# Behind the last linear scores: rotary keys next to the query latent, weights rounded ahead of tanh, the late gates' products first

## The chip, the cores and the metric

The kernel runs on one core of one Trainium2 chip. The metric is the device time of one execution in microseconds (us); the median of three runs is given, and lower is better. A profile is one more execution, taken with the hardware profiler.

## The reference

One transformer block for 512 tokens of width 1024, in float32. A norm and one wide linear layer give eleven pieces; a gated linear attention (GLA, 4 heads, two directions) and a latent attention (MLA, 8 heads) use them, and two gates mix the two. Then come an output layer, a second norm and a two-layer MLP.

```python
proj = rmsnorm(h, g_mix) @ w_in
(gq, gk, gv, gr, z_gf, z_gb, cq, ckv, kr, z_ma, z_mb) = split(proj)
y_gla = gla_branch(gq, gk, gv, gr, z_gf, z_gb, ...)       # scores, masked, times v, both directions
y_mla = mla_branch(cq, ckv, kr, positions, ...)
    # q = rmsnorm(cq) @ w_uq, its last 32 columns of each head rotated by the position
    # k_nope, v = rmsnorm(ckv) @ w_ukv;  k_rope = rope(kr), one for all heads
    # softmax(q k^T / sqrt(96)) v
merged = sigmoid(z_ma) * y_gla + sigmoid(z_mb) * y_mla
h = h + merged @ w_out
h = h + square(relu(rmsnorm(h) @ w_ff1)) @ w_ff2
out = rmsnorm(h)
```

## The kernel before

Tokens lie along the free axis (512) and features on the 128 partitions. Every float32 product is made of three matmuls (`mm3`, lines 88 to 90): each operand is split into a rounded part (h) and a remainder (l), and h·h, h·l and l·h are summed in PSUM. `split` (lines 92 to 94) makes the two parts: ScalarE rounds (line 93), then VectorE, or GpSimd where a caller says so, subtracts (line 94). Weights come through a stage of three SBUF buffers ("wf"): SyncE requests the next weight when the buffer's last reader is done.

PSUM holds two sets of four banks. The set "mm" takes products, "at" takes scores and the linear attention's outputs. A product that finds no free bank makes TensorE wait until the last reader of the oldest one is done.

The program runs in stages: the first linear layers, the linear attention head by head, the latents between them, then the latent attention (32 steps of scores, softmax, transposes and values), the output layer, and the MLP. The stage that matters here begins behind the scores of the last linear head (h = 3; `sc = gla_scores(...)`). Each engine works through its instructions in program order: the calls to `in_program_order` pin ScalarE, VectorE and TensorE to the order in which the code is written, with only TensorE moved in a few places. So what an engine does next is what the code says next, and one instruction that waits holds all behind it on its engine.

In this stage the code does the following, with names as in the profile:

- `zb5 = proj_run(...)` is a gate product; `gated` (lines 368 to 374) multiplies it by R, the reciprocal norm of each token, on VectorE (line 371), and makes tanh of half of it on ScalarE (line 373). tanh needs another function table than the sine before it (`ACT_TABLE_LOAD`).
- `cq_.normed()` splits the query latent (cqhl, lines 801 to 805); `rotary.tables()` makes sin and cos (lines 837, 838).
- `rotary_begin()` loads and splits two weights for the rotary queries (wr0, wr1), in two stage buffers.
- `ckv_.diagonals()` and `ckv_.spread()` prepare the norm of the key/value latent (ckvr, ckvdg, then ckvrs in PSUM); `ckv_.normed()` applies it and splits the result (ckvc, ckvhl).
- `begin(C_ZB + 6 * P, "zb6")` loads and splits the weights of gate 6; `begin(... "zb7")` those of gate 7.
- `gla_turn` transposes a finished linear head (y) and copies it out on ScalarE (yg, line 753); `gla_out` is the product of the last linear head (gla3o); `gla_squares` makes its squares on ScalarE (line 729), `gla_gated` the gated output on VectorE (grb, grc, line 740).
- `rotary_k()` rotates the keys on VectorE (lines 871 to 874), splits them (kbuf) and has SyncE copy them to three other key buffers (line 881).
- `rotary_q()` rotates the queries (roa, rob, ro; lines 860 to 862), and `up_units(0)` makes queries (wq0, uq, q), keys (wk0, uk) and values (uv) of the first two attention heads, a piece at each `next(units)`; the second piece asks SyncE for the copies of the rotary queries (line 1024).

On TensorE the order is: zb5, y, gla3o, ckvrs, the two rotary query products (ro), zb6, uq, uk, uv in two halves, zb7, the first attention scores (s).

Of the kernel before, what the change touches and what calls it, by code (L numbers as in the profile page):

```python
# [18 lines left out]
P = 128  # L19
# [16 lines left out]
C_ZA, C_ZB = 3776, 4800  # L36
# [20 lines left out]
def tile_block(ctx: ExitStack, tc: tile.TileContext, t, out: bass.AP):  # L57
# [6 lines left out]
    def tl(shape, dt, tag, bufs, name):  # L64
        serial[0] += 1
        return sb.tile(shape, dt, tag=tag, bufs=bufs, name=f"{name}_{serial[0]}")

    def u2(name, dt=F32, shape=(P, S)):
        return tl(list(shape), dt, "u2", 29, name)

    def u4(name, dt=F32R, shape=(P, 2, S)):
        return tl(list(shape), dt, "u4", 26, name)

    def sm(name, n=4, dt=F32):
        return tl([P, n], dt, "sm", 24, name)

    def ps(tag, name):
        serial[0] += 1
        return pp.tile([P, S], F32, tag=tag, bufs=4, name=f"{name}_{serial[0]}")
# [4 lines left out]
    def raw(x):  # L84
        return x.bitcast(F32)

    def mm3(acc, lh, ll, rh, rl, start, stop, onto=False):
        nc.tensor.matmul(acc, lh, rh, start=start, stop=False, skip_group_check=onto)  # L88
        nc.tensor.matmul(acc, lh, rl, start=False, stop=False, skip_group_check=onto)  # L89
        nc.tensor.matmul(acc, ll, rh, start=False, stop=stop, skip_group_check=onto)  # L90

    def split(hi, lo, src, rest=nc.vector):
        nc.scalar.activation(hi, src, AF.Copy)  # L93
        rest.tensor_tensor(lo, src, raw(hi), op=ALU.subtract)  # L94
# [12 lines left out]
    def traced():  # L107
        return len(nc.cur_bb.bb.instructions)
# [102 lines left out]
    def stage(nk, nw, name):  # L211
        wf = tl([P, nk, nw], F32, "wf", 3, f"{name}f")
        return wf

    def halves(nk, nw, name):
        wh = tl([P, nk, nw], F32R, "wh", 4, f"{name}h")
        wl = tl([P, nk, nw], F32R, "wl", 4, f"{name}l")
        return wh, wl
# [12 lines left out]
    def proj_begin(w, col, name, tag="mm"):  # L231
        wh, wl = weights(w[:, col : col + P], name)
        return wh, wl, ps(tag, name)

    def begin_late(col, name, tag="mm", w=None):

        wf = stage(KD, P, name)
        nc.sync.dma_start(wf, (w_in if w is None else w)[:, col : col + P].rearrange("(k p) w -> p k w", p=P))
        wh, wl = halves(KD, P, name)
        nc.scalar.activation(wh, wf, AF.Copy)  # L240

        def lows():
            nc.vector.tensor_tensor(wl, wf, raw(wh), op=ALU.subtract)

        return (wh, wl, ps(tag, name)), lows

    def proj_run(begun, src, half=None, ks=range(KD)):
        wh, wl, acc = begun
        c = slice(0, S) if half is None else slice(half * 256, half * 256 + 256)
        for k in ks:  # L250
            mm3(acc[:, c], wh[:, k, :], wl[:, k, :], src[k][:, 0, c], src[k][:, 1, c], k == 0, k == KD - 1)
        return acc
# [56 lines left out]
    xT = [u4(f"xT{k}") for k in range(KD)]  # L309
# [57 lines left out]

    def gated(acc, name):

        z = u2(f"z{name}")  # L370
        nc.vector.tensor_tensor(z, acc, R, op=ALU.mult)  # L371
        th = u2(f"t{name}")
        nc.scalar.activation(th, z, AF.Tanh, scale=0.5)  # L373
        return z, th

    def qk_normed(h, x, acc):
        n = u2(f"{'gq' if x == 0 else 'gk'}n{h}")
# [8 lines left out]
    g2 = [gated(f_accs[2 + x], f"b{x}")[1] for x in range(2)]  # L386
# [338 lines left out]
    def gla_squares(h, os):  # L725
        tot = sm(f"gla{h}ss")
        for i, o in enumerate(os):
            junk = u2(f"gla{h}sq")
            nc.scalar.activation(junk[:, 0:GDV], o, AF.Square, accum_out=tot[:, i : i + 1])
        nc.gpsimd.tensor_scalar(tot, tot, 1.0 / GDV, EPS, op0=ALU.mult, op1=ALU.add)  # L730
        nc.gpsimd.tensor_tensor(tot, tot, mhalf.to_broadcast([P, NT]), op=ALU.pow)
        nc.gpsimd.tensor_tensor(tot, tot, r_x, op=ALU.mult)
        return tot

    def gla_gated(h, os, rs):

        half, at = h // 2, (h % 2) * GDV
        for i, o in enumerate(os):
            g = g1[i, half][:, at : at + GDV]
            nc.vector.scalar_tensor_tensor(g, o, rs[:, i : i + 1], g, op0=ALU.mult, op1=ALU.mult)  # L740

    def gla_turn(h):

        half, at = h // 2, (h % 2) * GDV
        for dv in range(2):
            f = 2 * h + dv
            tp = ps("mm", f"y1{f}")
            for i in range(NT):
                nc.tensor.transpose(
                    tp[:, i * P : (i + 1) * P], g1[i, half][:, at + dv * P : at + (dv + 1) * P], ident  # L750
                )
            y = u2(f"yg{f}")
            nc.scalar.activation(y, tp, AF.Copy, scale=gla_gain[:, f : f + 1])
            y1.append(y)


    class Latent:
# [4 lines left out]
        def begin(self, j):  # L762
            self.begun[j] = proj_begin(w_in, self.col + j * P, f"{self.name}{j}")
# [77 lines left out]
    def rotary_begin():  # L841
        res = []
        for x in range(2):
            wf = stage(3, P, f"wr{x}")
            lo = NOPE + x * HALF
            for k in range(3):
                nc.sync.dma_start(
                    wf[:, k, :].rearrange("p (h e) -> p h e", h=MH), w_uq[:, k, :, lo : lo + HALF]
                )
            wh, wl = halves(3, P, f"wr{x}")  # L850
            split(wh, wl, wf)
            res.append((wh, wl))
        return res

    def rotary_q(accs):
        res = []
        for x in range(2):
            a, b = u2(f"roa{x}"), u2(f"rob{x}")
            ta, tb = (cos, sin) if x == 0 else (sin, cos)
            nc.vector.scalar_tensor_tensor(a, accs[0], QK_SCALE, ta, op0=ALU.mult, op1=ALU.mult)  # L860
            nc.vector.scalar_tensor_tensor(b, accs[1], QK_SCALE, tb, op0=ALU.mult, op1=ALU.mult)
            nc.vector.tensor_tensor(a, a, b, op=ALU.subtract if x == 0 else ALU.add)
            hl = u4(f"ro{x}")
            split(hl[:, 0, :], hl[:, 1, :], a)
            res.append(hl)
        return res

    def rotary_k():
        r = slice(64, 96)
        sgn = u2("krsin")  # L870
        nc.vector.tensor_scalar(sgn[r], sin[r], cst[r, K_SIGN : K_SIGN + 1], None, op0=ALU.mult)
        nc.vector.tensor_tensor(kswap[r], kswap[r], sgn[r], op=ALU.mult)
        nc.vector.tensor_tensor(kr[r], kr[r], cos[r], op=ALU.mult)
        nc.vector.tensor_tensor(kr[r], kr[r], kswap[r], op=ALU.add)
        res = []
        for b in range(4):
            kb = u4(f"kbuf{b}")
            if b == 0:
                split(kb[r, 0, :], kb[r, 1, :], kr[r])
            else:  # L880
                nc.sync.dma_start(raw(kb[r]), raw(res[0][r]))
            res.append(kb)
        return res
# [258 lines left out]
    ckv_, cq_ = Latent(C_CKV, 2, V_KV, "ckv"), Latent(C_CQ, 3, V_Q, "cq")  # L1142
# [73 lines left out]
    for h in range(GH - 1):  # L1216
# [5 lines left out]
        acc = latent.products(j)  # L1222
        if h < 2:
            w_b, lows = begin_late(C_GQ + (h + 2) * P, f"gq{h + 2}")
# [15 lines left out]
        os = gla_out(h, sc)  # L1240
        scaled_qk.within("b", gate.parts)
        rs = gla_squares(h, os)
# [11 lines left out]
        else:  # L1254
            zb = begin(C_ZB + 4 * P, "zb4")
# [4 lines left out]
            w_b = begin(C_ZB + 5 * P, "zb5")  # L1260
            zb = proj_run(zb, xT)

    h = GH - 1
    sc = gla_scores(*scaled_qk.parts())
    ckv_.sums()
    zb5 = proj_run(w_b, xT)
    cq = cq_.normed()
    cos, sin = rotary.tables()
    wr = rotary_begin()
    g2.append(gated(zb, "b4")[1])  # L1270
    g2.append(gated(zb5, "b5")[1])
    ckv_.diagonals()
    zb = begin(C_ZB + 6 * P, "zb6")
    gla_turn(h - 1)
    os = gla_out(h, sc)
    kbuf = rotary_k()
    ckv_.spread()
    rs = gla_squares(h, os)
    ckv = ckv_.normed()
    accs = [up_T(*w, cq, f"ro{x}") for x, w in enumerate(wr)]  # L1280
    units = up_units(0)
    next(units)
    ro = rotary_q(accs)
    gla_gated(h, os, rs)
    zb = proj_run(zb, xT)
    next(units)
    g2.append(gated(zb, "b6")[1])
    zb = begin(C_ZB + 7 * P, "zb7")
    first_units = traced()
    for _ in units:  # L1290
        pass
    first_units = first_units, traced()
    at = traced()
    zb = proj_run(zb, xT)
    last_gate = at, traced()
    g2.append(gated(zb, "b7")[1])
    in_program_order(fixed, SPLITTERS)
# [3 lines left out]
    units = up_units(1)  # L1301
# [5 lines left out]
    for n in range(4 * MH + LAG_C - 1):  # L1307
# [19 lines left out]
        if n in (6, 14):  # L1327
            units = up_units(n // 8 + 2)
# [4 lines left out]
        b = n - LAG_B  # L1333
# [45 lines left out]
    for i in range(NT):  # L1379
        r = u4(f"h{i}", F32, (P, D))  # L1380
# [186 lines left out]
    y, z = merged_sums(last, nc.vector)  # L1567
# [81 lines left out]
    for qd in range(NQ):  # L1649
# [14 lines left out]
        for n, m in enumerate(ORDER):  # L1664
# [4 lines left out]
            if m == 2:  # L1669
                accs, begin = [ps("mm", f"gw{qd}{rb}") for rb in range(2)], True  # L1670
# [3 lines left out]
            else:  # L1674
                accs, begin = (zs_, m == 5) if m in (5, 3) else (xs_, m == 1)
# [46 lines left out]
```

## Time and profile before

| | us |
|---|---|
| three runs | 763.59, 764.57, 764.74 (median 764.57) |
| the profiled execution | 766.85 |
| its span, first to last instruction | 764.8 |
| TensorE busy (matmul) | 751.8 (98%) |
| VectorE busy | 586.4 (77%) |
| ScalarE busy | 461.6 (60%) |
| GpSimd busy | 165.3 (22%) |
| mean granted clock of TensorE | 0.991 |

Engines are named PE (TensorE matmul), PEld (its weight loads), DVE (VectorE), ACT (ScalarE), POOL (GpSimd) and SP (SyncE, which requests transfers). L371 is line 371 of the kernel before. A timeline row has start, duration, engine, line, operation, output <- inputs, the shape and the number of merged instructions, and in brackets the idle time before it with who ended it. Buffer numbers are left out of names, so zb stands for each of the gates, and its neighbours tell which. Matmuls overlap: a row's duration is longer than the distance to the next one.

### The profile page before, as it was taken

How to read it: one execution, taken by the hardware profiler on the slowest of the kernel's cores; microseconds unless marked ns; L12 is line 12 of the kernel's file. 1: busy time of each engine (PE TensorE's matmuls, PEld its weight loads, DVE VectorE, ACT ScalarE, POOL GpSimd, SP SyncE). 2: the span in 40 equal slices, each digit the busy share in tenths (PEclk: the TensorE clock that was granted, in tenths of full speed). 3: DMA queues.
4: the chain of work that ended last, by engine and by line, in shares of the span. 5: the costliest groups of instructions: out<-in, count | busy, mean ns of one | idle time of the engine just before them, and what ended most of it. 6: DMA issues, size and time to landing. Idle time of an engine off the chain costs nothing.

```text
span 764.8 us, 10256 instructions
## 1 busy us (share of the span) xinstructions
PE 751.8 (98%) x3720; PEld 636.1 (83%) x3720; DVE 586.4 (77%) x850; ACT 461.6 (60%) x780; POOL 165.3 (22%) x238
## 2 busy tenths in 40 slices
PE   9999999999999997999999999999999999999996
PEld 7888887889889886889888988888888888888885
DVE  7777888789787575798997876965887478848795
ACT  7556565577567473898866775435653556346634
POOL 0722110262562512117662100000000000000014
PEclk9999999999999997999999999999999999999999
DMA  9849581711222233227989421363115510650002
GB/s 311 253 132 230 164 176 57 130 29 32 78 56 37 40 80 90 66 56 205 251 205 241 138 84 55 111 186 89 56 56 186 144 34 22 193 166 0 28 1 110
DMA packets 94306, 87.59 MB, mean 115 GB/s; under 512 B 15696, under 2 KB 66896, under 8 KB 94256
## 3 DMA queue, kind: packets, MB, share of 16 engines
q1 hardware_dynamic: 87760, 74.33, 32.5%
q0 software_dynamic: 6208, 12.32, 9.1%
q8 instruction: 29, 0.48, 0.3%
q10 hardware_dynamic: 288, 0.28, 0.1%
q14 instruction: 21, 0.17, 0.1%
HBM read 83.25 MB, written 2.10 MB: 112 GB/s over the span
## 4 chain that ended last, share of the span: by engine, by line
PE 90%; DVE 4%; ACT 3%; issue 1%; POOL 0%; POOLq 0%; ACTq 0%; DVEq 0%
PE f L88 8%; PE f L89 8%; PE f L90 8%; PE gx L88 4%; PE gx L89 4%; PE gx L90 4%; PE first L330 3%; PE gz L88 2%; PE gz L89 2%; PE gz L90 2%; PE tp L1081 1%; PE zb L88 1%; PE zb L89 1%; PE zb L90 1%; PE wox L88 1%
## 5 line engine op out<-in xcount | busy, mean ns | idle before, releaser
L1661 POOL DMA_DIRECT2D gfin<-in_g_final x1 | 0.6, 628 | 284.0 <-PE f L90 284.0
L951 DVE TENSOR_TENSOR w<-w,w 128x1024 f32<-128x1024 f32 x32 | 38.7, 1221 | 0.3
L1061 DVE TENSOR_REDUCE top<-s 128x1 f32<-128x512 f32 x32 | 21.8, 681 | 2.9 <-PE s L90 2.6
L1066 ACT ACTIVATE e<-s,top 128x512 f32<-128x512 f32 x32 | 22.0, 689 | 2.6 <-DVE top L1061 2.4
L94 DVE TENSOR_TENSOR pT<-tp,pT 128x512 fp32r<-128x512 f32 x32 | 21.6, 681 | 2.4 <-ACT pT L93 2.2
L1388 DVE TENSOR_TENSOR h<-h,gx 128x512 f32<-128x512 f32 x32 | 21.5, 682 | 1.9 <-PE gx L90 1.8
L93 ACT ACTIVATE pT<-tp 128x512 fp32r<-128x512 f32 x32 | 18.9, 597 | 3.2 <-PE tp L1081 3.1
L1081 PE MATMUL tp<-ident,e 128*128 128x128 f32 x128 | 19.3, 274 | 0.4 <-ACT e L1072 0.2
L88 PE MATMUL av<-pT,v 128*128 128x256 f32 x64 | 18.9, 296 | 0.0
L93 ACT ACTIVATE ghb<-y 128x512 fp32r<-128x512 f32 x16 | 10.1, 633 | 14.0 <-DVE y L897 14.0
L1454 ACT ACTIVATE fa<-f 128x512 f32<-128x512 f32 x32 | 18.5, 578 | 0.0
L1081 PEld LDWEIGHTS tp<-ident,e 128*128 128x128 f32 x128 | 15.1, 140 | 3.9 <-ACT e L1072 0.8
L89 PE MATMUL av<-pT,v 128*128 128x256 f32 x64 | 18.2, 285 | 0.0
L90 PE MATMUL av<-pT,v 128*128 128x256 f32 x64 | 18.2, 284 | 0.0
L540 ACT ACTIVATE bds<-bd 128x512 f32<-128x512 f32 x4 | 2.4, 598 | 20.9 <-PE bd L536 20.9
L93 ACT ACTIVATE b_00h<-w 128x1024 fp32r<-128x1024 f32 x7 | 7.4, 1059 | 12.6 <-PE gz L90 6.0
L373 ACT ACTIVATE tb<-zb 128x512 f32<-128x512 f32 x8 | 4.9, 631 | 16.5 <-DVE zb L371 16.5
L93 ACT ACTIVATE b_20h<-w 128x1024 fp32r<-128x1024 f32 x7 | 7.4, 1059 | 12.1 <-PE gz L90 6.0
L93 ACT ACTIVATE b_10h<-w 128x1024 fp32r<-128x1024 f32 x7 | 7.4, 1060 | 12.1 <-PE gx L90 6.0
L88 PE MATMUL s<-kbuf,q 96*128 96x512 f32 x32 | 14.2, 444 | 0.1
L1463 ACT ACTIVATE px<-fa 128x256 f32<-128x256 f32 x32 | 13.4, 418 | 1.0
L947 POOL DMA_DIRECT2D w<-in_w_out x10 | 12.2, 1398 | 6.5 <-DVE bo60l L94 5.3
(1731 smaller groups left out, 2956.2 us busy)
## 6 DMA issues: line engine op xcount, KB each, us to landing
w<-in_w_ff SPq DMA_DIRECT2D x64, 256.0 KB, 3.4
w<-in_w_out POOLq DMA_DIRECT2D x10, 512.0 KB, 9.0
grw<-in_w_in SPq DMA_DIRECT2D x8, 512.0 KB, 8.5
zaw<-in_w_in SPq DMA_DIRECT2D x8, 512.0 KB, 6.5
gvw<-in_w_in SPq DMA_DIRECT2D x8, 512.0 KB, 4.5
w<-in_w_out SPq DMA_DIRECT2D x16, 256.0 KB, 6.2
x<-in_xt SPq DMA_DIRECT2D x8, 256.0 KB, 5.3
vw<-in_w_first SPq DMA_DIRECT2D x8, 256.0 KB, 5.4
```

The source lines that it names most:

```text
L88: nc.tensor.matmul(acc, lh, rh, start=start, stop=False, skip_group_check=onto)
L89: nc.tensor.matmul(acc, lh, rl, start=False, stop=False, skip_group_check=onto)
L90: nc.tensor.matmul(acc, ll, rh, start=False, stop=stop, skip_group_check=onto)
L93: nc.scalar.activation(hi, src, AF.Copy)
L94: rest.tensor_tensor(lo, src, raw(hi), op=ALU.subtract)
L330: nc.tensor.matmul(f_accs[i], a[:, i * P : (i + 1) * P], b, start=k == 0 and x == 0, stop=k == KD - 1 and x == 2)
L951: nc.vector.tensor_tensor(wq[dst][g], wq[x][g], wq[y][g], op=op)
L1061: nc.vector.tensor_reduce(top, acc, axis=AX.X, op=ALU.max, negate=True)
L1066: nc.scalar.activation(e, acc, AF.Exp, bias=top, accum_out=tot[:, qt % 2 : qt % 2 + 1])
L1081: nc.tensor.transpose(tp[:, k * P : (k + 1) * P], e[:, k * P : (k + 1) * P], ident)
L1388: nc.vector.tensor_tensor(hc, hc, acc, op=op)
L1454: nc.scalar.activation(a, acc, AF.Relu)
```

## The change

The code of the stage is written in another order; nothing is added to what is computed and nothing left out. `gated` is cut into its product and its tanh, and `rotary_k` into rotation and split, so that the parts can stand apart. TensorE's and GpSimd's orders stay as they are.

```diff
     cq = cq_.normed()
     cos, sin = rotary.tables()
+    late = [over_rms(acc, f"b{f}") for f, acc in ((4, zb), (5, zb5))]
+    rotary_k()
+    ckv_.diagonals()
     wr = rotary_begin()
-    g2.append(gated(zb, "b4")[1])
-    g2.append(gated(zb5, "b5")[1])
-    ckv_.diagonals()
     zb = begin(C_ZB + 6 * P, "zb6")
+    kbuf = rotary_k_split()
+    g2 += [half_tanh(z, f"b{f}") for f, z in ((4, late[0]), (5, late[1]))]
     gla_turn(h - 1)
     os = gla_out(h, sc)
-    kbuf = rotary_k()
+    rs = gla_squares(h, os)
     ckv_.spread()
-    rs = gla_squares(h, os)
     ckv = ckv_.normed()
     accs = [up_T(*w, cq, f"ro{x}") for x, w in enumerate(wr)]
     units = up_units(0)
     next(units)
     ro = rotary_q(accs)
+    zb = over_rms(proj_run(zb, xT), "b6")
+    next(units)
+    w_b = begin(C_ZB + 7 * P, "zb7")
     gla_gated(h, os, rs)
-    zb = proj_run(zb, xT)
-    next(units)
-    g2.append(gated(zb, "b6")[1])
-    zb = begin(C_ZB + 7 * P, "zb7")
+    g2.append(half_tanh(zb, "b6"))
     first_units = traced()
     for _ in units:
         pass
     first_units = first_units, traced()
     at = traced()
-    zb = proj_run(zb, xT)
+    zb = proj_run(w_b, xT)
     last_gate = at, traced()
     g2.append(gated(zb, "b7")[1])
```

The new functions hold what `gated` and `rotary_k` held:

```python
    def over_rms(acc, name):
        z = u2(f"z{name}")
        nc.vector.tensor_tensor(z, acc, R, op=ALU.mult)
        return z

    def half_tanh(z, name):
        th = u2(f"t{name}")
        nc.scalar.activation(th, z, AF.Tanh, scale=0.5)
        return th
```

VectorE behind the query latent, before (wr0l and wr1l are the remainders of the rotary query weights, zb4 and zb5 the gate products, ckvr to ckvdg the diagonals, krsin and kswap the first steps of the rotary keys):

```order
L94 TENSOR_TENSOR wr0l_502_2573<-wr0f_500_2568,wr0h_501_2572 128x384
L94 TENSOR_TENSOR wr1l_505_2581<-wr1f_503_2576,wr1h_504_2580 128x384
L371 TENSOR_TENSOR zb4_506_2584<-zb4_475_2412,R_82 128x512
L371 TENSOR_TENSOR zb5_508_2588<-zb5_482_2455,R_82 128x512
L789 TENSOR_TENSOR ckvr_494_2524<-ckvr_494_2524,r_x_80 128x4
L791 CAST ckvrh_510_2593<-ckvr_494_2524 128x4
L792 TENSOR_TENSOR ckvrl_511_2594<-ckvr_494_2524,ckvrh_510_2593 128x4
L292 TENSOR_TENSOR ckvdg_512_2597<-ident_61,ckvrh_510_2593 128x512
L292 TENSOR_TENSOR ckvdg_512_2597<-ident_61,ckvrl_511_2594 128x512
L94 TENSOR_TENSOR zb6l_515_2603<-zb6f_513_2600,zb6h_514_2602 128x1024
L871 TENSOR_SCALAR krsin_523_2671<-sin_499_2565,gvec_78 32x512
L872 TENSOR_TENSOR kswap_66_353<-kswap_66_353,krsin_523_2671 32x512
```

And the same place now:

```order
L375 TENSOR_TENSOR zb4_500_2568<-zb4_475_2412,R_82 128x512
L375 TENSOR_TENSOR zb5_501_2570<-zb5_482_2455,R_82 128x512
L878 TENSOR_SCALAR krsin_502_2572<-sin_499_2565,gvec_78 32x512
L879 TENSOR_TENSOR kswap_66_353<-kswap_66_353,krsin_502_2572 32x512
L880 TENSOR_TENSOR kr_65_352<-kr_65_352,cos_498_2564 32x512
L881 TENSOR_TENSOR kr_65_352<-kr_65_352,kswap_66_353 32x512
L796 TENSOR_TENSOR ckvr_494_2524<-ckvr_494_2524,r_x_80 128x4
L798 CAST ckvrh_503_2578<-ckvr_494_2524 128x4
L799 TENSOR_TENSOR ckvrl_504_2579<-ckvr_494_2524,ckvrh_503_2578 128x4
L292 TENSOR_TENSOR ckvdg_505_2582<-ident_61,ckvrh_503_2578 128x512
L292 TENSOR_TENSOR ckvdg_505_2582<-ident_61,ckvrl_504_2579 128x512
L94 TENSOR_TENSOR wr0l_508_2590<-wr0f_506_2585,wr0h_507_2589 128x384
```

The gate products and the four steps of the rotary keys stand first; the rotary query weights' remainders, which stood first, follow the diagonals, and behind them come the remainders of zb6 and of the keys (kbuf).

ScalarE in the same place, before (wr1h and zb6h are rounded weights, tb4 and tb5 the tanh, yg the transposed head, kbuf0 the rounded rotary keys, gla3sq the squares):

```order
L93 ACTIVATE wr1h_504_2580<-wr1f_503_2576 128x384
L373 ACT_TABLE_LOAD
L373 ACTIVATE tb4_507_2586<-zb4_506_2584 128x512
L373 ACTIVATE tb5_509_2590<-zb5_508_2588 128x512
L93 ACTIVATE zb6h_514_2602<-zb6f_513_2600 128x1024
L753 ACTIVATE yg4_518_2612<-y14_517_2607,gla_gain_350 128x512
L753 ACTIVATE yg5_520_2619<-y15_519_2614,gla_gain_350 128x512
L93 ACTIVATE kbuf0_524_2676<-kr_65_352 32x512
L729 ACTIVATE gla3sq_530_2689,gla3ss_529_2688<-gla3o0_521_2621 128x256
```

And now:

```order
L93 ACTIVATE wr1h_510_2597<-wr1f_509_2593 128x384
L93 ACTIVATE zb6h_513_2603<-zb6f_512_2601 128x1024
L93 ACTIVATE kbuf0_516_2608<-kr_65_352 32x512
L380 ACT_TABLE_LOAD
L380 ACTIVATE tb4_520_2617<-zb4_500_2568 128x512
L380 ACTIVATE tb5_521_2619<-zb5_501_2570 128x512
L760 ACTIVATE yg4_523_2626<-y14_522_2621,gla_gain_350 128x512
L760 ACTIVATE yg5_525_2633<-y15_524_2628,gla_gain_350 128x512
L736 ACTIVATE gla3sq_529_2686,gla3ss_528_2685<-gla3o0_526_2635 128x256
```

The weights of zb6 and the keys are rounded ahead of the table load and tanh; the keys stood behind yg.

VectorE again, behind the rotary queries, before (ro1 ends the rotary queries, grb and grc are the gated head, zb6 the gate's product by R, zb7l the remainder of gate 7's weights, q00 and q01 the query remainders of the first two heads):

```order
L94 TENSOR_TENSOR ro1_549_2761<-roa1_547_2756,ro1_549_2761 128x512
L740 SCALAR_TENSOR_TENSOR grb_108_490<-gla3o0_521_2621,gla3ss_529_2688,grb_108_490 128x256
L740 SCALAR_TENSOR_TENSOR grb_109_491<-gla3o0_521_2621,gla3ss_529_2688,grb_109_491 128x256
L740 SCALAR_TENSOR_TENSOR grc_110_492<-gla3o1_522_2622,gla3ss_529_2688,grc_110_492 128x256
L740 SCALAR_TENSOR_TENSOR grc_111_493<-gla3o1_522_2622,gla3ss_529_2688,grc_111_493 128x256
L371 TENSOR_TENSOR zb6_552_2798<-zb6_516_2606,R_82 128x512
L94 TENSOR_TENSOR zb7l_556_2805<-zb7f_554_2802,zb7h_555_2804 128x1024
L98 SCALAR_TENSOR_TENSOR q00_550_2792<-uq0_558_2809,q00_550_2792 64x512
L98 SCALAR_TENSOR_TENSOR q01_551_2795<-uq0_558_2809,q01_551_2795 64x512
```

And now:

```order
L94 TENSOR_TENSOR ro1_549_2761<-roa1_547_2756,ro1_549_2761 128x512
L375 TENSOR_TENSOR zb6_550_2788<-zb6_515_2607,R_82 128x512
L94 TENSOR_TENSOR zb7l_555_2799<-zb7f_553_2796,zb7h_554_2798 128x1024
L747 SCALAR_TENSOR_TENSOR grb_108_490<-gla3o0_526_2635,gla3ss_528_2685,grb_108_490 128x256
L747 SCALAR_TENSOR_TENSOR grb_109_491<-gla3o0_526_2635,gla3ss_528_2685,grb_109_491 128x256
L747 SCALAR_TENSOR_TENSOR grc_110_492<-gla3o1_527_2636,gla3ss_528_2685,grc_110_492 128x256
L747 SCALAR_TENSOR_TENSOR grc_111_493<-gla3o1_527_2636,gla3ss_528_2685,grc_111_493 128x256
L98 SCALAR_TENSOR_TENSOR q00_551_2790<-uq0_558_2809,q00_551_2790 64x512
L98 SCALAR_TENSOR_TENSOR q01_552_2793<-uq0_558_2809,q01_552_2793 64x512
```

The gate's product and the remainder of gate 7's weights stand ahead of the four gatings; on ScalarE the rounding of zb7 stands ahead of the tanh of zb6. Among SyncE's requests one place changes: zb7's weights stood ahead of the three key copies (kbuf) and now stand behind them. The requests for the rotary queries stay where they were.

More of the change, by code (lines that the diff above doesn't have):

```diff
@@ L368, in gated @@
     def gated(acc, name):
+        z = over_rms(acc, name)
+        return z, half_tanh(z, name)
+    def over_rms(acc, name):
         z = u2(f"z{name}")
         nc.vector.tensor_tensor(z, acc, R, op=ALU.mult)
+        return z
+    def half_tanh(z, name):
         th = u2(f"t{name}")
         nc.scalar.activation(th, z, AF.Tanh, scale=0.5)
-        return z, th
+        return th
     def qk_normed(h, x, acc):
@@ L874, in rotary_k, with rotary_k_split @@
         nc.vector.tensor_tensor(kr[r], kr[r], kswap[r], op=ALU.add)
+    def rotary_k_split():
+        r = slice(64, 96)
         res = []
```

## The prediction

> **What bounds the kernel now.** I read three views in this order: the waits of TensorE, the granted clock by stretch, and the timeline of the stage behind the last linear scores. First the waits of TensorE over the whole span (waited for: us in total, times, longest):
>
> ```profile
> PE zb L88 <- DVE q L98: 2.2, 1, 2.2
> PE uv L88 <- DVE zb L371: 1.7, 1, 1.7
> ...
> PE tp L1081 <- ACT e L1072: 0.2, 1, 0.2
> ```
>
> Before its last instruction TensorE hardly waits but in two places, and both lie in this stage. So whatever is won there shortens the span, if nothing late follows. The same two in the timeline (start, duration, what is computed, and in brackets the idle time and who ended it), with the start of the attention scores behind them:
>
> ```profile
> 292.05 0.28 PE L90 MATMUL uv<-wk0h,ckvhl 128*128 128x256 f32 x1
> 294.07 0.39 PE L88 MATMUL uv<-wk0h,ckvhl 128*128 128x256 f32 x1 [1.74 <-DVE zb L371]
> 299.04 0.76 PE L88 MATMUL zb<-xT,zb7h 128*128 128x512 f32 x1 [2.23 <-DVE q L98]
> 307.17 0.40 PE L88 MATMUL s<-kbuf,q 96*128 96x512 f32 x1
> ```
>
> The second half of the values (uv) waits for the PSUM bank that gate zb6 holds until VectorE multiplies it by R. Gate zb7 waits for the bank of uq, free when VectorE has made the second head's query remainder (q L98). Then the clock, in stretches of 3.4 us (stretch, length, busy us of PE, PEld, DVE, ACT and POOL with counts, then granted clock, DMA share, GB/s):
>
> ```profile
> 290.90:294.30 3.40, 1.66 (x15) 1.46 (x14) 2.86 (x6) 0.42 (x2) 0.00 (x0) 1.00 0.55 156
> 294.30:297.70 3.40, 2.51 (x12) 2.21 (x11) 1.82 (x2) 2.00 (x4) 0.00 (x0) 0.50 0.12 19
> 301.10:304.50 3.40, 3.40 (x9) 2.63 (x9) 1.18 (x2) 1.66 (x6) 2.67 (x5) 0.50 0.28 40
> 304.50:307.20 2.70, 2.70 (x13) 2.21 (x13) 0.00 (x0) 0.00 (x0) 0.56 (x1) 0.99 0.71 239
> ```
>
> After the first wait the clock is at half until 304.5, so the 24 matmuls of zb7 take 307.17 - 299.04 = 8.13 us. Gate zb6, also 24 matmuls, shows their price at full clock, with two more starts on which the sum rests:
>
> ```profile
> 270.42 0.39 PE L90 MATMUL zb<-xT,zb5l 128*128 128x512 f32 x1
> 278.20 0.39 PE L90 MATMUL ro<-cqhl,wr0l 128*128 128x512 f32 x1
> 281.83 0.39 PE L88 MATMUL zb<-xT,zb6h 128*128 128x512 f32 x1
> 287.27 0.39 PE L88 MATMUL uq<-cqhl,wq0h 128*128 128x512 f32 x1
> ```
>
> 287.27 - 281.83 = 5.44 us, so the half clock costs zb7 2.7 us. Both waits end on VectorE, which is why its row is what the change has to shorten.
>
> **The change part by part.** VectorE's row in this stage:
>
> ```profile
> 268.08 1.89 DVE L805 TENSOR_TENSOR cqhl<-cqc,cqhl 128x512 fp32r<-128x512 f32 x3
> 271.84 0.56 DVE L94 TENSOR_TENSOR wr0l<-wr0f,wr0h 128x384 fp32r<-128x384 f32 x1 [1.86 <-ACT wr0h L93]
> 272.78 1.28 DVE L371 TENSOR_TENSOR zb<-zb,R 128x512 f32<-128x512 f32 x2
> 276.97 1.23 DVE L94 TENSOR_TENSOR zb6l<-zb6f,zb6h 128x1024 fp32r<-128x1024 f32 x1 [1.23 <-ACT zb6h L93]
> 278.23 0.48 DVE L871 TENSOR_SCALAR krsin<-sin,gvec 32x512 f32<-32x512 f32 x1
> 281.44 0.68 DVE L94 TENSOR_TENSOR kbuf<-kr,kbuf 32x512 fp32r<-32x512 f32 x1 [0.69 <-ACT kbuf L93]
> 282.15 1.29 DVE L801 TENSOR_TENSOR ckvc<-ckvc,ckvrs 128x512 f32<-128x512 f32 x2
> 284.89 0.69 DVE L860 SCALAR_TENSOR_TENSOR roa<-ro,cos 128x512 f32<-128x512 f32 x1
> ```
>
> It idles 1.86 + 1.23 + 0.69 us on ScalarE here. The new order fills the first gap and removes the others. VectorE is free at 268.08 + 1.89 = 270.0. The product of zb5 needs the matmul that ends at 270.42 + 0.39 = 270.8, so the two products (0.64 each) end at 271.5. Rotary keys (from 278.23 to the gap that ends at 281.44, so to 280.75, 2.5 us): 274.0. The diagonals (from the products' end, 274.06, to the gap that ends at 276.97, so 1.7 us): 275.7. Two rotary weight remainders (271.84 to 272.78, 1.0 us): 276.7. The remainder of zb6 (1.23): 277.9; of the keys (0.68): 278.6; the two latent products (1.29): 279.9. Then ScalarE decides, whose rows are:
>
> ```profile
> 270.68 0.71 ACT L838 ACTIVATE cos<-turns,half_pi 128x512 f32<-128x512 f32 x1
> 273.55 1.28 ACT L373 ACT_TABLE_LOAD   x1 [1.33 <-DVE zb L371]
> 274.84 1.16 ACT L373 ACTIVATE tb<-zb 128x512 f32<-128x512 f32 x2
> 276.84 1.25 ACT L753 ACTIVATE yg<-y,gla_gain 128x512 f32<-128x512 f32 x2
> 281.43 0.38 ACT L729 ACTIVATE gla3sq<-gla3o 128x256 f32<-128x256 f32 x1
> 283.00 1.16 ACT L803 ACTIVATE ckvhl<-ckvc 128x512 fp32r<-128x512 f32 x2
> 284.48 1.11 ACT L93 ACTIVATE wk0h<-wk0f 128x128 fp32r<-128x128 f32 x4
> ```
>
> Sine and cosine are ready at 271.4, in time. Rounding the keys now stands ahead of the table load and waits for them at 274.0: keys (the gap of 0.69 that they made on VectorE) 274.7, load 276.0, both tanh 277.1, both yg 278.4, squares (281.43 to 283.00) 279.9. There the latent's rounding begins; it began at 283.00. The first rotary query product began 1.89 us behind it, so it begins at 281.8, in place of 284.89, and its partner's matmuls end just then (281.83 in TensorE's rows). That is 3.1 us won.
>
> The table load is now on this chain. [...]
>
> Rounding zb6's weights ahead of tanh is worth nothing by itself: they were ready at 278.2 and are needed at 281.83. If that cover went, TensorE would wait for each late microsecond. That the copies of the rotary queries are requested earlier is worth nothing either; they keep their place among SyncE's transfers, behind wk1f. What moves on SyncE is a cost: stage buffers come free later. The rows (issue; then KB each, us to landing):
>
> ```profile
> 273.99 0.37 SPq L1007 DMA_DIRECT2D wk0f<-in_w_ukv  x1
> wk0f<-in_w_ukv SPq DMA_DIRECT2D x1, 384.0 KB, 5.4
> zb7f<-in_w_in SPq DMA_DIRECT2D x1, 512.0 KB, 4.0
> ```
>
> wk0f goes out 1.6 us behind the end of wr0l (272.40), now 276.3, so at 277.9, and lands at 283.3. Its four roundings (1.11) then hold ScalarE until 284.4, while the first rotary difference, three VectorE steps behind 281.8, is ready at 283.9: 0.5 us lost. A landing faster than 4.9 us makes that nothing, a slower one adds all of itself; I take the row's 5.4. zb7f now stands behind the three key copies, which wait for 278.6; going out near 281, it lands near 285, needed at 288. The late halves of the old row follow:
>
> ```profile
> 291.16 0.69 DVE L94 TENSOR_TENSOR ro<-roa,ro 128x512 fp32r<-128x512 f32 x1 [0.70 <-ACT ro L93]
> 291.77 0.87 DVE L740 SCALAR_TENSOR_TENSOR grb<-gla3o,gla3ss,grb 128x256 f32<-128x256 f32 x2
> 293.34 0.68 DVE L371 TENSOR_TENSOR zb<-zb,R 128x512 f32<-128x512 f32 x1
> 295.72 1.23 DVE L94 TENSOR_TENSOR zb7l<-zb7f,zb7h 128x1024 fp32r<-128x1024 f32 x1 [1.70 <-ACT zb7h L93]
> 296.86 0.68 DVE L98 SCALAR_TENSOR_TENSOR q<-uq,q 64x512 fp32r<-64x512 f32 x1
> 298.20 0.69 DVE L98 SCALAR_TENSOR_TENSOR q<-uq,q 64x512 fp32r<-64x512 f32 x1 [0.66 <-ACT q L97]
> ```
>
> Rotary queries take 284.89 to 291.85, 7.0 us: 281.8 + 7.0 + 0.5 = 289.3. Now zb6 comes first (0.6): 289.9, before TensorE reaches uv's second half at 292.05 + 0.12 = 292.2. **The first wait, 1.74 us, is gone.** Then zb7's remainder (1.23), whose rounding ScalarE does meanwhile, so that the 1.70 us wait goes: 291.1. The four gatings (291.77 to 293.34, 1.6): 292.7. The two query remainders (296.86 to 298.89, 2.0): 294.7. zb7 followed them by 0.15: **294.85 instead of 299.04, 4.2 us earlier.** uv's 12 matmuls at 0.12 end at 293.6, so a wait of about 1.25 us stays where 2.23 was.
>
> If that does not drop the clock, zb7 takes 5.44 instead of 8.13 us, 2.7 us more. **Sum: 4.2 + 2.7 = 6.9 us.** The profiled execution, 766.85 us with a span of 764.8, would become 760.0; the median of the runs lies 2.28 below it, so 764.57 - 6.9 = 757.7. If wk0f lands early: 757.2. If nothing of the second wait stayed (zb7 at 293.6): 299.04 - 293.6 + 2.7 = 8.1, so 756.4.
>
> **Rivals.** *The clock drops on the wait that stays.* For: one wait of 1.74 us did it, in a stretch with 1.66 of 3.40 us busy. Against: 1.25 us leaves a stretch nearly two thirds busy. Between 0.2 and 1.74 us this trace shows no wait behind which the clock could be read with certainty. The clock came back after one stretch that was all busy, so half clock would last 3.4 to 6.8 us and cost half of that, 1.7 to 3.4: 759.4 to 761.1. [...]
>
> *Late transfers take the wait's place.* wk0f or zb7f lands 3 us later, among the key copies: from 282.8 for wk0f and 288 for zb7f each microsecond goes to zb7's start. 757.7 + 2.5 and up to 3.4 of clock: 760 to 764.
>
> *Given back in the attention.* If that were bound by VectorE or ScalarE, an earlier start would be lost again: 763.1 to 766.1. Against: both stood idle ahead of it, VectorE over 5 us:
>
> ```profile
> 307.37 0.69 DVE L371 TENSOR_TENSOR zb<-zb,R 128x512 f32<-128x512 f32 x1 [5.09 <-PE zb L90]
> ```
>
> *Slower.* The remainder wr0l, moved behind rotary keys and diagonals, is ready at 276.3; TensorE reads it at 278.20. From a slip of 1.9 us, say of the tables or the key transfers, TensorE waits, and all of the chain behind it too. To be 1.5 us slower than before the wait must be 6.9 + 1.5 = 8.4 us, or 5.0 with the clock fallen: 766.1 and more. Nothing in the rows is that late.
>
> **How the numbers follow.** Forecast (756.4 to 759.2, clock up): 0.72. Clock drops: 0.13. Late transfers: 0.07. Given back: 0.05. Slower: 0.03. A measurement of this kernel tells about 0.2%, 1.5 us. Faster: 0.72 + 0.13 + 0.07 = 0.92 (the edge of late transfers within it), same 0.05, slower 0.03. The range takes the first two cases, and 0.4 us below them for the spread of single runs (763.59 to 764.74 before): 756.0 to 761.1.
>
> **What would show it.** Right: uv never waits, one wait of about 1.25 us ahead of zb7, granted clock 1.00 throughout, first rotary product about 3 us earlier, roundings of wk0 close behind its landing. Wrong: a wait ahead of ro or zb6, a clock of 0.50 behind uv, or waits of TensorE in the attention that weren't there.

## The result, and the profile after

| | before | after |
|---|---|---|
| median of the runs | 764.65 us (763.59 to 764.74, 4 runs) | 758.15 us (757.73 to 758.25, 4 runs) |
| the profiled execution | 766.85 | 758.25 |
| its span | 764.8 | 756.4 |
| mean granted clock | 0.991 | 0.998 |

The ratio of the medians is 0.9917, its 95% interval 0.99 to 0.9934: 5.0 to 7.6 us faster. 757.7 was forecast. First the waits of TensorE after the change (waited for: us in total, times, longest):

```profile
PE warm L320 <- POOL ident masks.py:199: 1.5, 1, 1.5
PE zb L88 <- DVE q L98: 0.6, 1, 0.6
PE zax L88 <- DVE zac L688: 0.4, 1, 0.4
PE tp L1091 <- ACT e L1082: 0.2, 1, 0.2
```

The wait of uv is gone, that of zb7 is 0.6 in place of 2.2 us, and no row is new in the attention. The stage in TensorE's timeline, from the first transposition of the finished head (y), through uv's second half and zb7, to the first scores:

```profile
269.62 0.38 PE L756 MATMUL y<-ident,grb 128*128 128x128 f32 x2
...
291.07 0.28 PE L88 MATMUL uv<-wk0h,ckvhl 128*128 128x256 f32 x1
...
292.39 0.28 PE L90 MATMUL uv<-wk0h,ckvhl 128*128 128x256 f32 x1
293.25 0.47 PE L88 MATMUL zb<-xT,zb7h 128*128 128x512 f32 x1 [0.58 <-DVE q L98]
298.80 0.40 PE L88 MATMUL s<-kbuf,q 96*128 96x512 f32 x1
```

And where the stage began before:

```profile
270.65 0.38 PE L749 MATMUL y<-ident,grb 128*128 128x128 f32 x2
```

From y to zb7 it is 293.25 - 269.62 = 23.63 us; before, 299.04 - 270.65 = 28.39: **4.76 us less**. zb7 itself, to the first scores, takes 5.55 in place of 8.13: **2.58 less**. Together 7.34 us. From the first scores to the end of the span it is 756.4 - 298.8 = 457.6 us after and 764.8 - 307.2 = 457.6 before: nothing of the gain is given back. The span is 8.4 us shorter; the 1.03 that are left lie ahead of the stage, in code that is the same in both. They arise in the first 8 us of the program, at the first matmuls of 512 columns, here before:

```profile
5.07 2.05 PE L330 MATMUL first<-xT,first0h 128*128 128x512 f32 x4
6.91 1.42 PE L330 MATMUL first<-xT,first0l 128*128 128x512 f32 x4
8.17 1.09 PE L330 MATMUL first<-xT,first0h 128*128 128x512 f32 x4
```

and after:

```profile
4.97 1.38 PE L330 MATMUL first<-xT,first0h 128*128 128x512 f32 x4
6.19 1.11 PE L330 MATMUL first<-xT,first0l 128*128 128x512 f32 x4
7.13 2.00 PE L330 MATMUL first<-xT,first0h 128*128 128x512 f32 x8
```

The first eight take 8.17 - 5.07 = 3.10 us before and 7.13 - 4.97 = 2.16 after, and from there to the stage the two run alike. The change can't have made this: with the same early code, the run with both edits (below) took 3.09 us for these eight and began the stage at 270.50. The profile gives a clock of 1.00 there in all of them, so why they take longer stays open. For comparison with the forecast's times, 1.03 us has to be added to every start of the profile after.

The granted clock, in stretches that hold the remaining wait and zb7 up to 298.0 (stretch, length, busy us of PE, PEld, DVE, ACT and POOL with counts, then clock, DMA share, GB/s):

```profile
290.00:294.00 4.00, 3.42 (x26) 3.14 (x25) 3.13 (x6) 1.33 (x3) 0.00 (x0) 1.00 0.60 107
294.00:296.00 2.00, 2.00 (x10) 1.65 (x9) 1.49 (x3) 1.98 (x5) 0.00 (x0) 1.00 0.34 57
296.00:298.00 2.00, 2.00 (x11) 1.65 (x10) 0.49 (x1) 0.98 (x4) 1.95 (x3) 1.00 0.00 0
```

It stays at 1.00, to the end of zb7 too, where it was 0.50 for some 10 us. VectorE's row, which the change was to shorten:

```profile
269.81 0.69 DVE L375 TENSOR_TENSOR zb<-zb,R 128x512 f32<-128x512 f32 x1 [0.28 <-PE zb L90]
...
272.37 0.68 DVE L881 TENSOR_TENSOR kr<-kr,kswap 32x512 f32<-32x512 f32 x1
...
274.77 0.55 DVE L94 TENSOR_TENSOR wr0l<-wr0f,wr0h 128x384 fp32r<-128x384 f32 x1
275.71 1.22 DVE L94 TENSOR_TENSOR zb6l<-zb6f,zb6h 128x1024 fp32r<-128x1024 f32 x1
276.95 0.68 DVE L94 TENSOR_TENSOR kbuf<-kr,kbuf 32x512 fp32r<-32x512 f32 x1
277.67 1.28 DVE L808 TENSOR_TENSOR ckvc<-ckvc,ckvrs 128x512 f32<-128x512 f32 x2
280.56 0.68 DVE L867 SCALAR_TENSOR_TENSOR roa<-ro,cos 128x512 f32<-128x512 f32 x1
...
283.65 0.90 DVE L94 TENSOR_TENSOR ro<-roa,ro 128x512 fp32r<-128x512 f32 x1 [1.08 <-ACT ro L93]
...
287.17 0.69 DVE L94 TENSOR_TENSOR ro<-roa,ro 128x512 fp32r<-128x512 f32 x1 [0.70 <-ACT ro L93]
287.78 0.68 DVE L375 TENSOR_TENSOR zb<-zb,R 128x512 f32<-128x512 f32 x1
288.38 1.22 DVE L94 TENSOR_TENSOR zb7l<-zb7f,zb7h 128x1024 fp32r<-128x1024 f32 x1
289.51 0.87 DVE L747 SCALAR_TENSOR_TENSOR grb<-gla3o,gla3ss,grb 128x256 f32<-128x256 f32 x2
...
291.08 0.67 DVE L98 SCALAR_TENSOR_TENSOR q<-uq,q 64x512 fp32r<-64x512 f32 x1
292.41 0.69 DVE L98 SCALAR_TENSOR_TENSOR q<-uq,q 64x512 fp32r<-64x512 f32 x1 [0.66 <-ACT q L97]
```

The three gaps on ScalarE that the prediction named (1.86, 1.23, 0.69 us) are gone, as is the 1.70 ahead of zb7's remainder. zb6's product, for which uv had waited, ends at 288.46; uv's second half starts at 291.07. What is still in the way of zb7 is the last row: the second query remainder, behind the gatings. ScalarE's row where the forecast put its largest doubt:

```profile
273.09 0.63 ACT L93 ACTIVATE kbuf<-kr 32x512 fp32r<-32x512 f32 x1 [0.96 <-DVE kr L881]
273.73 1.28 ACT L380 ACT_TABLE_LOAD   x1
...
278.65 1.18 ACT L810 ACTIVATE ckvhl<-ckvc 128x512 fp32r<-128x512 f32 x2
...
281.96 1.13 ACT L93 ACTIVATE wk0h<-wk0f 128x128 fp32r<-128x128 f32 x4 [1.72 <-DMA wk0f<-in_w_ukv]
283.00 0.62 ACT L93 ACTIVATE ro<-roa 128x512 fp32r<-128x512 f32 x1
```

ScalarE waits 1.72 us for the weights of the keys, and the rounding of the first rotary query stands behind them: the difference it reads is done at 281.87 + 0.69 = 282.56, it starts at 283.00.

### The profile page after: what moved, and what is told of

Its sections match the earlier page's. It is cut to its first block, busy times and chain, and to the rows that moved or that the text cites. A ratio compares the mean times of both kernels' runs of the same rounds, so it can differ in the third digit from the quotient of the medians.

```text
span 756.4 us, 10256 instructions
## 1 busy us (share of the span) xinstructions
PE 746.8 (99%) x3720; PEld 632.4 (84%) x3720; DVE 586.1 (77%) x850; ACT 461.5 (61%) x780; POOL 165.0 (22%) x238
## 4 chain that ended last, share of the span: by engine, by line
PE 92%; DVE 4%; ACT 2%; issue 1%; DMA 1%; POOL 0%; POOLq 0%; DVEq 0%; ACTq 0%
PE f L90 8%; PE f L88 8%; PE f L89 8%; PE gx L88 4%; PE gx L90 4%; PE gx L89 4%; PE first L330 3%; PE gz L90 2%; PE gz L88 2%; PE gz L89 2%; PE tp L1091 1%; PE zb L88 1%; PE zb L90 1%; PE zb L89 1%; PE wox L88 1%; PE wox L89 1%
## 5 line engine op out<-in xcount | busy, mean ns | idle before, releaser
L636 POOL DMA_DIRECT2D gvw<-in_w_in x4 | 4.8, 1227 | 39.1 <-DVE gvw L641 30.7
```

## The experiments

**Theory.** VectorE's order sets when zb7 starts; the clock, which fell to 0.50 behind the wait of 1.74 us before, stays up behind the shorter one that is left, so the change wins twice, by the waits and by the clock. **Rivals:** the gain comes from the early half or the late half alone; the clock follows something other than the waits; the loss of 0.5 us to late weights, or the wait that is left, decides more (or less) than the sum gave it.

In the comparisons below, before was run 21, 15 and 7 times more, with medians of 764.78, 764.75 and 764.8. These times fall into groups by the mean clock: 763.5 to 763.9 at 0.997 to 0.998, 764.1 to 765.2 at 0.993 to 0.996 (most), and 766.6 to 766.8 at 0.991 to 0.992. The profiled execution, 766.85 at 0.991, belongs to the last. This matters for the clock term. Only one execution of each version was profiled; of the others, time and mean clock are known, and where the text says that the clock fell in them, it goes by these two.

### The late half alone

The early block as before; gate zb6 ahead of the gatings as changed.

```diff
+    wr = rotary_begin()
     late = [over_rms(...) ...]
-    rotary_k()
+    g2 += [half_tanh(...) ...]
     ckv_.diagonals()
-    wr = rotary_begin()
     zb = begin(C_ZB + 6 * P, "zb6")
-    kbuf = rotary_k_split()
-    g2 += [half_tanh(...) ...]
     gla_turn(h - 1)
     os = gla_out(h, sc)
-    rs = gla_squares(h, os)
+    rotary_k()
+    kbuf = rotary_k_split()
     ckv_.spread()
+    rs = gla_squares(h, os)
```

> Only the late half of the change: zb6's product, zb7's weights and then the four gatings, with everything ahead of the rotary queries as before. Theory (the gain is the whole of VectorE's row, and the clock): zb6's bank is free 1.6 us earlier, so the wait ahead of uv falls from 1.74 us to about 0.3; zb7 begins only 1.8 us earlier, so the wait ahead of it grows from 2.2 to about 3.3 us, the clock falls to half behind it for 3.4 to 6.8 us, and of 6.5 us about 1.8 are won: 762.9 us (761.9 to 763.6). Rival (the product of zb6 ahead of the gatings is the whole gain, the rest lies off the path): 758.2 us.

Measured: 763.42 us (761.52 to 764.09, 10 runs), ratio 0.9975 (0.9964 to 0.9986). Two rows of TensorE's timeline and three stretches of it:

```profile
291.39 0.39 PE L88 MATMUL uv<-wk0h,ckvhl 128*128 128x256 f32 x1 [0.17 <-DVE zb L375]
...
296.12 0.77 PE L88 MATMUL zb<-xT,zb7h 128*128 128x512 f32 x1 [3.05 <-DVE q L98]
```

```profile
293.00:296.10 3.10, 0.08 (x1) 0.01 (x1) 2.41 (x6) 1.18 (x2) 0.00 (x0) 0.91 0.59 108
296.10:299.50 3.40, 3.38 (x9) 2.74 (x10) 2.57 (x4) 2.75 (x8) 0.59 (x1) 0.58 0.35 58
299.50:303.00 3.50, 3.50 (x18) 2.85 (x17) 0.00 (x0) 0.34 (x2) 2.66 (x5) 1.00 0.43 117
```

The first wait shrinks to 0.17 us, but what it gave goes into the second, which grows from 2.23 to 3.05: from y to zb7 it is 26.58 us, 1.81 less than before. The clock falls in that one wait, half a microsecond ahead of its end (0.91 in the first stretch), and zb7 takes 6.87 us. One execution of the ten, 761.52 us at 0.997, stands apart from the others (762.6 to 764.09 at 0.994 to 0.996): in it the clock seems to have stayed up. So the late half by itself is worth 1.4 us; the rival that it carries the change is refuted.

### The early half alone

```diff
     ro = rotary_q(accs)
+    gla_gated(h, os, rs)
     zb = over_rms(proj_run(zb, xT), "b6")
     next(units)
-    w_b = begin(C_ZB + 7 * P, "zb7")
-    gla_gated(h, os, rs)
     g2.append(half_tanh(zb, "b6"))
+    w_b = begin(C_ZB + 7 * P, "zb7")
```

> Only the early half: gate products, rotary keys and diagonals first, weights and keys rounded ahead of tanh; behind the rotary queries the gatings come first again, then zb6's product, and tanh ahead of zb7's rounding. Theory: the rotary queries end 3.1 us earlier, so zb6's bank is free 1 us before uv needs it and the first wait is gone; the rounding of zb7 behind tanh puts the query remainders 1.75 us later than in the whole change, the wait ahead of zb7 is about 2.4 us in place of 0.6, and the clock falls on it: 758.15 + 1.75 + 1.7 to 3.4 = 761.6 to 763.3 us, or 759.9 if the clock stays up. Rival (the zb6 product's place is the whole gain): about 764.7 us.

Measured: 761.64 us (760.32 to 762.32, 6 runs), ratio 0.9959 (0.9943 to 0.9974). Its waits, and the stretches ahead of and at zb7:

```profile
PE zb L88 <- DVE q L98: 2.0, 1, 2.0
```

```profile
293.30:295.30 2.00, 0.03 (x2) 0.03 (x1) 1.31 (x3) 1.19 (x2) 0.00 (x0) 1.00 0.34 63
295.30:300.80 5.50, 5.50 (x24) 4.58 (x25) 2.54 (x4) 3.10 (x8) 2.71 (x5) 1.00 0.46 77
```

The early half takes the first wait away by itself. With the late half undone zb7 starts 1.39 us later than after the whole change, behind a wait of 1.97. In the profiled execution (760.32 us, mean clock 0.997) the clock stayed up and zb7 took 5.54; the five others, at 0.995 to 0.996, took 761.59 to 762.32. So with a wait of 1.97 us in the profile the clock fell in five executions of six, not in all. The halves are worth 1.4 and 3.1 us alone and 6.5 together. The clock is a part of the 2.0 us between: it fell in nine executions of ten with the late half, in five of six with the early one, and in none of four with both. By the next experiment it is worth about 1.25 us of the median; what the rest is isn't shown, and the intervals of the three ratios leave room for it.

### Before, with TensorE kept busy in its waits

Here nothing is moved. Seven and fourteen matmuls into a bank that nobody reads stand in the two waits, and add work that the reference doesn't have.

```diff
+    def fill(n):
+        if not fills:
+            fills.append(ps("at", "fill"))
+        for _ in range(n):
+            nc.tensor.matmul(fills[0], xT[0][:, 0, 0:P], xT[1][:, 0, :], start=True, stop=True)
...
             vs.append(hl)
+            if pr == 0:
+                fill(7 if j == 0 else 14)
             yield
```

> The kernel before, its order unchanged, with 7 matmuls of 128x512 more on TensorE ahead of uv's second half and 14 more ahead of zb7, into a bank that nobody reads. They lie inside the two waits, so TensorE is busy nearly all the time; VectorE's row and so the starts of uv and zb7 stay as they were. Theory (half clock is 2.7 us of the gain): granted clock 1.00 throughout the stage, zb7's 24 matmuls take 5.4 us, 2.7 us are won although work is added: 762.0 us. Rival (the clock costs nothing, only the waits do): 764.7 us or a little more.

Measured: 763.53 us (763.07 to 764.44, 10 runs, clock 0.997 to 0.999), ratio 0.9978 (0.9967 to 0.9989). The filling matmuls, zb7 and the first scores, then two stretches:

```profile
291.16 1.78 PE L1003 MATMUL fill<-xT,xT 128*128 128x512 f32 x7
...
294.58 3.36 PE L1003 MATMUL fill<-xT,xT 128*128 128x512 f32 x14
298.02 0.47 PE L88 MATMUL zb<-xT,zb7h 128*128 128x512 f32 x1
...
303.59 0.40 PE L88 MATMUL s<-kbuf,q 96*128 96x512 f32 x1
```

```profile
294.00:298.00 4.00, 3.95 (x21) 3.04 (x20) 2.60 (x4) 2.34 (x4) 0.00 (x0) 1.00 0.15 32
298.00:301.40 3.40, 3.38 (x15) 2.80 (x16) 2.58 (x4) 2.75 (x8) 0.58 (x1) 1.00 0.58 101
```

From y to zb7 it is 28.39 us, to the hundredth what it was before, and zb7 takes 5.57 in place of 8.13. This separates the two terms: with the waits filled and nothing else changed the clock stays at 1.00 from 294.00 to 301.40, where before it was at 0.50 from 294.33 on, and the clock alone costs 2.56 us in the profiled pair. The median gained only 1.25 us (764.78 to 763.53), half of what the theory expected: the profiled execution of before lost more to the clock than most of its others. Their mean clocks fit this. In the profile the clock was at half for 10.24 us, from 294.33 to 304.57 (read in stretches of 0.25 us), which is three times the 3.41 us that it was at half behind a single wait, with the late half alone and with four idle products (below). By an estimate from these lengths, 3.41 us at half of 764 us lower the mean clock by 0.002 and 10.24 us by 0.007: from 0.998, that gives 0.996 for most executions of before and 0.991 for the profiled one.

### The query remainders ahead of the gatings

The last thing ahead of zb7 is put first; the whole change besides.

```diff
     w_b = begin(C_ZB + 7 * P, "zb7")
+    next(units)
     gla_gated(h, os, rs)
```

> The whole change, and the query remainders of the first two heads moved ahead of the four gatings on VectorE. Theory (zb7 waits only for the bank that these remainders free): they end 1.6 us earlier, the 0.58 us that zb7 still waits are gone and the time falls by that: 757.6 us. Rival (the gatings, now later, hold two banks of the scores and the head that is transposed next): a new wait ahead of the attention scores, 758.2 us or more.

Measured: 757.52 us (757.31 to 757.9, 4 runs), ratio 0.9899 (0.988 to 0.9917). The last matmul of uv, zb7 behind it, and the first scores:

```profile
292.39 0.28 PE L90 MATMUL uv<-wk0h,ckvhl 128*128 128x256 f32 x1
292.51 0.40 PE L88 MATMUL zb<-xT,zb7h 128*128 128x512 f32 x1
...
297.98 0.40 PE L88 MATMUL s<-kbuf,q 96*128 96x512 f32 x1
```

zb7 follows uv without a wait, and no wait is new elsewhere. From y to the first scores it is 28.36 us, 0.82 less than after the change; the median is 0.63 lower. In this profile the weights of the keys also landed sooner (3.9 us from issue in place of 5.0), and the rotary queries ended 0.33 us earlier; by itself that would have left about 0.25 of the 0.58 us, as in the next run (0.24), so the order removes the rest. It has the lowest median here, but its range touches those of the change and of the two versions below.

### The rotary query weights ahead of the diagonals

This frees wk0's stage buffer sooner, so that its transfer starts earlier.

```diff
-    ckv_.diagonals()
     wr = rotary_begin()
+    ckv_.diagonals()
```

> The whole change, with the remainders of the two rotary query weights moved from behind the diagonals to ahead of them. Theory (the later stage buffers cost 0.44 us, since wk0 lands late and its roundings hold up that of the rotary queries on ScalarE): wk0 is requested 1.8 us earlier, its roundings follow the one of wq0 at once, zb7 begins 0.4 us earlier and 0.1 to 0.2 of the 0.58 us wait is left: 757.7 us. The diagonals end 1 us later, 0.3 us ahead of the product that reads them. Rival (the transfers' place is covered): 758.15 us; or the diagonals are late: 758.3 us and a wait ahead of the latent's spread.

Measured: 757.93 us (757.83 to 758.49, 5 runs), ratio 0.9915 (0.9902 to 0.9929). ScalarE's roundings of wk0 and of the first rotary query:

```profile
280.12 1.14 ACT L93 ACTIVATE wk0h<-wk0f 128x128 fp32r<-128x128 f32 x4
...
282.68 0.63 ACT L93 ACTIVATE ro<-roa 128x512 fp32r<-128x512 f32 x1 [1.41 <-DVE roa L869]
```

ScalarE no longer waits for the weights, and the rotary query waits for VectorE alone, as it should. The stage is 28.81 us, 0.37 less than after the change. By time alone the two can't be told apart (the change ran 757.73 to 758.25). Nor is the 0.44 us that it removes always paid: with the weights left behind the diagonals, in the profiles of the run above and of the one with a single idle product below, the rotary queries ended 0.33 and 0.42 us earlier in the stage than in the profile of the change. There the weights of the keys took 3.9 and 4.5 us from issue to landing, and 5.0 in the change, with the same requests ahead of them: the landing differs from execution to execution.

Both edits together:

> Both: weights' remainders ahead of the diagonals, and the query remainders ahead of the gatings. Theory (with the query remainders first nothing is waited for in this stage): no more than with the query remainders alone, 757.5 us, since what VectorE does earlier is not waited for. Rival (VectorE's row still bounds): 757.1 us.

Measured: 757.79 us (757.31 to 758.4, 4 runs), ratio 0.9912 (0.9899 to 0.9926). From y to the first scores it is 28.36 us, the same as with the query remainders alone: once TensorE waits for nothing, earlier weights move nothing.

### How long a wait brings the clock down

Idle products on VectorE ahead of the query remainders, whose output nobody reads, lengthen the one wait that is left.

```diff
     gla_gated(h, os, rs)
+    idle = u2("idle")
+    for _ in range(n):
+        nc.vector.tensor_tensor(idle, R, R, op=ALU.mult)
```

With one:

> The whole change, with one more VectorE product of 128x512 (R times R into a buffer that nobody reads) ahead of the query remainders: the wait ahead of zb7 grows from 0.58 to about 1.2 us, the size that was forecast for the change. If the clock stays up at such a wait: 758.15 + 0.6 = 758.75 us at a mean clock of 0.998. If it falls: 1.7 to 2.7 us more, 760.4 to 761.5, and 0.995.

With two:

> The whole change, with two more VectorE products of 128x512 (R times R into a buffer that nobody reads) ahead of the query remainders: the wait ahead of zb7 grows from 0.58 to about 1.8 us. Clock up in all runs: 758.15 + 1.2 = 759.35 us at a mean clock of 0.998. [...]

With four:

> The same with four such products: a wait of about 3.0 us. Clock up: 760.55 us. Clock falling in nearly all runs: 761.5 to 763.3 us at 0.994 to 0.996.

| idle products | wait, us | zb7, us | median (runs), us | ratio (interval) | mean clock of the runs |
|---|---|---|---|---|---|
| none (the change) | 0.58 | 5.55 | 758.15 (4) | 0.9917 (0.99 to 0.9934) | 0.998 |
| 1 | 0.77 | 5.52 | 758.55 (4) | 0.9921 (0.9905 to 0.9938) | 0.997 to 0.998 |
| 2 | 1.50 | 5.53 | 759.89 (4) | 0.9937 (0.9924 to 0.9951) | 0.998 to 0.999 |
| 4 | 3.03 | 7.18 | 763.01 (10) | 0.9979 (0.997 to 0.9988) | 0.994 to 0.996 |

With one, the wait came out shorter than expected because the rotary queries ended 0.4 us earlier in that execution. The stretches around zb7 with four:

```profile
293.00:296.00 3.00, 0.04 (x1) 0.07 (x1) 2.27 (x5) 1.18 (x2) 0.00 (x0) 1.00 0.41 67
296.00:299.00 3.00, 3.00 (x8) 2.33 (x9) 2.31 (x4) 2.42 (x6) 0.25 (x1) 0.52 0.00 0
299.00:301.00 2.00, 2.00 (x9) 1.62 (x8) 0.20 (x1) 0.68 (x3) 2.00 (x4) 0.87 0.24 13
```

With waits of 0.58, 0.77 and 1.50 us in the profiles the clock stays up in every run (0.997 to 0.999). With two, from y to the first scores it is 30.08 us, 0.90 more than after the change, which is the wait (1.50 - 0.58 = 0.92). The two profiled executions differ by 1.83 (760.08 and 758.25), since in the one with two idle products the stage also began at 270.52, 0.90 later; the medians differ by 1.74, and where the stage began in the other executions isn't known. With four, at 3.03 us, the clock falls in every run (0.994 to 0.996); in the profile it was at half from 296.10 to 299.51, 3.41 us. The forecast had to guess between 0.2 and 1.74; its 1.25 us lay on the safe side, and so did the 0.58 that came.

## Why the prediction was right

- **Where the gain comes from.** Right: VectorE's row set the start of zb7. With 1.03 added, its steps ended as forecast: products 271.5, keys 274.1 (274.0), zb6's remainder 278.0 (277.9), the latent products 280.0 (279.9), the squares 279.7 (279.9).
- **The weights that land later.** Right: wk0f took 5.0 us (5.4 taken) and cost 0.44 us (0.5). The earlier weights removed that loss from the profile, and other profiles with the change's order show that it varies.
- **The first wait.** Right: gone, and by the early half alone.
- **The start of zb7.** Mis-sized by 0.6 us: 294.28 in place of 294.85, so 4.76 us earlier and not 4.2, and the wait that is left is 0.58 and not 1.25 (0.16 of this lies in the count: the profile's waits begin at the end of uv's last matmul, the sum's 0.12 after its start). No step was wrong; the rotary queries began 0.2 us earlier and took some 0.2 less, and VectorE's rows behind them overlap a little more than the sum, which added them, allowed.
- **The clock.** Right that it stays up (1.00 to the end of zb7), and that this shortens zb7: kept at 1.00 without moving anything, it made zb7 as short, 5.57 us against 5.55. For the profiled execution the size was right as well, 2.58 us against 2.7. Taken off the median it was too much: by the filled version, the median of before loses about 1.25 us to the clock. The step that failed is the subtraction of a term of one execution, which was among the slowest, from the median of others. The forecast hit since the two errors have opposite signs: 4.2 + 2.7 = 6.9 forecast, 4.76 + 1.25 = 6.0 by the parts, 6.5 (5.0 to 7.6) measured. That it came within 0.5 us is in part luck, and the interval can't tell 6.0 from 6.9.
- **The rivals.** *The clock drops on the wait that is left*: refuted at 0.58, and at 1.50 us too; with a wait of 1.97 us in the profile (early half alone) the clock fell in five executions of six. Its price was right at the low end: half clock for 3.41 us made zb7 1.3 us longer with the late half alone and 1.6 with four idle products (6.87 and 7.18 against 5.55), where 1.7 to 3.4 was taken. The 3.4 to 6.8 us at half clock behind it were the author's estimate; no profile shows 6.8: there it lasted 3.41 us twice and, before, 10.24. *Late transfers take the wait's place*: wk0f did so for 0.44 us, zb7f not at all. (By the prediction's own rows a landing of wk0f 3 us later adds 3.0 us to its sum and not 2.5, so its bounds should be 760.7 and 764.1.) *Given back in the attention*: refuted, 457.6 us from the first scores to the end in both. *Slower, by wr0l*: its remainder was ready at 275.3 (276.4 in the forecast's time) and TensorE waited for neither ro nor zb6.

## What to carry to other kernels

Where TensorE is 98% busy, look at its few waits one by one: put first on the releasing engine what it waits for, and what nobody waits for (here the gatings) behind. Here waits of 0.58 to 1.50 us cost their length alone; with one of 1.97 us the clock also fell in five executions of six, and with one of 3.0 us in nineteen of twenty. So shortening two waits together can bring more than the two apart (here 6.5 us, against 1.4 and 3.1). Before a term that was read in one profiled execution is taken off a median, compare that execution's time and mean clock with the other runs'.

## What the runs showed of the hardware

- The clock doesn't always fall after the same wait. A wait of 1.50 us lowered it in none of four executions. One of 1.74 us did in the profile of before (1.00 until 294.33, then 0.50). One of 1.97 us did in five executions of six, by time and mean clock, and one of 3.0 us in nineteen of twenty (late half alone and four idle products).
- The moment of the fall isn't a fixed time behind the start of the wait. Two waits of one length, 3.05 and 3.03 us, brought it 2.5 us into the wait (late half alone, at 295.53) and 0.1 us behind its end (four idle products, at 296.10); before, it came 0.3 us behind the end of the wait of 1.74 us. The stretch at half clock lasted 3.41 us in the first two and three times that, 10.24 us, in the last, where a second wait followed. What sets the moment, and why a wait lowers the clock in one execution and not in the next, isn't shown.
- The same program differs by 3 us from execution to execution: before took 763.5 to 763.9 us where its mean clock was 0.997 to 0.998, and 766.6 to 766.8 where it was 0.991 to 0.992. In the profiled one of these, 2.56 us lie in the clock of zb7, and its first eight wide matmuls took 0.94 us longer than those of the profile after, at a clock given as 1.00. So the mean clock doesn't tell all: with both edits, the two executions at 0.999 took 758.24 and 758.4 us, the two at 0.998 757.31 and 757.34. What decides which group an execution falls into stays open.
- The load of wk0 (384 KB) took from 3.4 to 5.4 us from issue to landing in these profiles. The order of the requests isn't all of it: with the same requests ahead of it it took 5.0, 4.5 and 3.9 us (the change, one idle product, query remainders first).
